# Query projection of a hybrid encoder: feature-major in a 3-pass split instead of token-major in fp32, rotary part through DRAM

## The chip, the cores and the metric

The kernel runs on one core of one Trainium2 chip. The metric is the device time of one execution in microseconds (us). TensorE (PE) multiplies, VectorE (DVE), ScalarE (ACT) and GpSimd (POOL) work element by element, SyncE (SP) issues DMAs; ACT and POOL issue some too. Each engine takes its instructions in the order in which they were written for it, and waits at the first that isn't ready.

## The reference

Two encoder layers for 256 prompt tokens and 8 streams of 16 sample tokens, so 384 token rows. A layer projects its input with `w_in`, feeds three head groups, projects their outputs with `w_out`, and ends in a SwiGLU block. The change touches the queries of group A, latent attention (8 heads, 64 plain and 32 rotary features each):

```python
q = einsum('btr,rf->btf', rmsnorm(cq, mla_q_norm), w_uq).reshape(B, T, 8, 96)
q_nope, q_pe = q[..., :64], rope(q[..., 64:], pos)
# prompt: s = (q_lat . ckv + q_pe . kpe) * 96 ** -0.5, softmax in a block-causal mask
# sample: the same over 256 cached rows and 16 new ones, q_lat = q_nope . w_uk
```

Group B is a gated delta rule (an inverse of small triangular matrices, then a recurrence over four chunks of 64 tokens), group C a convolution of width 31 over 256 channels.

## The kernel before

All activations that are multiplied with big weights stand feature-major, features on partitions and the 384 tokens along the free axis. The big products are made in a split of three passes: `split` writes a high part (fp32r, by ACT) and a low part (the rest, by DVE), and `g3` issues three fp32r matmuls, high x high, low x high and high x low. Small products are plain fp32, which the compiler makes two PE instructions each.

The order of the work is not that of the source. Each section opens with `at('name')`, which adds an offset from the table `PRI` to the priority of what follows, and a scheduler orders each engine's instructions by priority and readiness. `ENG` says which engine makes a copy or issues a DMA. So sections overlap: the convolution's 62 tap instructions a layer (`acc`, section `taps`, one DVE instruction each) are spread over DVE from the moment the convolution input is there until `cpost`.

The names that the prediction uses, in the order of a layer:
- `pt`, `pf`: PE products of `w_in`, token- or feature-major. `cq` is the query input; `ev_cq` takes its mean square (`rcq`, nine small DVE steps for the power of -1/2) and transposes it (`pcq`).
- `Tn`, `pr`: the 15 DVE steps of the triangular inverse; its result goes to DRAM (`scr`, SP) and comes back (`tc`, POOL), then PE products `pL`.
- `py`, `pkS`, `Sn`, `o`, `so`: the chunks of the recurrence; then the sample state's part, `pxs`, `pxt`, `pu`, `po`, `o2s`, `pgo`, `pS`. DVE scales the sample state by one long instruction, `S<-S,gv`.
- `queries(t)`, one for each tile of 128 tokens: six fp32 products `pq` of 384 columns (tokens stationary), a scaling with the norm factor to `qp` (ACT), the rotary part `rp` and `qp` (DVE), eight PE transposes `pqT`, copies to `qT` (ACT). For the sample tile also `qpe` and the products `pqL`.
- `scores` and `values` (`psc`, `mx`, `P`, `pPT`, `ppv`) for the prompt's eight head pairs; `past`, `s_scores` and `s_values` (`ppn`, `pkp`, `pss`, `mxs`, `E`, `Ps`, `pPs`, `poL`) for the eight streams.
- `cy`: the end of the convolution group; then `w_out` (`pw`).

Of the kernel before, what the change touches and what calls it, by code (L numbers as in the profile page):

```python
# [33 lines left out]
def _constants():
# [56 lines left out]
def encoder_step(ctx, tc, I, O):  # L91
# [251 lines left out]
    for L in range(depth):  # L343
# [487 lines left out]
        for t in range(3):  # L831
            pool.memset(kps[t], 0.0)
            if t < 2:
                pool.tensor_copy(kps[t][:, 32 + t:128:64], ctab[:, K_KP:K_KP + 1].to_broadcast([128, 2]))
# [164 lines left out]
        wq = []  # L999
        for k in range(3):  # L1000
            w = stm.tile([128, 1024], F32, name="wq", tag="wlo", bufs=NW)[:, 0:768]
            sp.dma_start(w, I['w_uq'][L][k * 128:k * 128 + 128, :])
            wq.append(w)
        qT = [None] * 3

        def queries(t):
            cT_, r = cqT[t]
            qp = tl(k2p, "qp", 1, 1024, "qp").rearrange("p (a c) -> p a c", a=4)
            e = pool if ENG.get('qpm', 'p') == 'p' else dve
            m = qp[:, :, 96:224].rearrange("p a (b c) -> p a b c", b=2)  # L1010
            e.memset(m[:, :, :, 0:32], 0.0)
            if t < 2:
                e.tensor_copy(m[:, :, :, t], ctab[:, None, K_QP:K_QP + 1].to_broadcast([128, 4, 2]))
            for hf in range(2):
                p = psum("pq", "gg"[hf])
# [337 lines left out]
```

## Time and profile before

| | us |
|---|---|
| median of 3 runs | 1084.95 (1084.43 to 1089.22) |
| the profiled execution, its own time | 1090.11 |
| its span, first to last instruction | 1088.0 |
| PE busy in the span | 1045.5 (96%) |
| DVE, ACT, POOL busy | 633.6 (58%), 470.1 (43%), 75.5 (7%) |
| mean granted TensorE clock | 0.987 of full speed |

The profiled execution took 5.2 us more than the median of the runs, and its span is 2.1 us shorter than its own time. A busy PE counts each matmul from its start to its modelled end, and successive ones overlap. Stages are read below as windows of the span; layer 0's mixing work ends at about 222 us, layer 1's at about 759 us, and the SwiGLU block follows each.

### The profile page before, as it was taken

The page shows a single profiled execution, that of the slowest core. Times are in us where ns is not written, and L with a number is a line of the kernel's source. Part 1 is how long each engine was busy: PE and PEld are TensorE (multiplying, and loading weights), DVE is VectorE, ACT ScalarE, POOL GpSimd, SP SyncE. Part 2 cuts the span into 40 slices and gives each one's busy share as a digit, 9 for nine tenths or more (in the row PEclk, how much of TensorE's full clock was granted, in tenths as well). Part 3 has the DMA queues.
Part 4 walks back from the last instruction along what each step waited for, and adds up shares of the span by engine and source line. Part 5 has one row for each costly group of instructions (what it writes and reads, how often), then busy time and mean ns, then how long its engine had stood idle before and what let it go on. Part 6 is the DMA issues. An engine that isn't in the chain of part 4 may idle for free.

```text
span 1088.0 us, 17535 instructions
## 1 busy us (share of the span) xinstructions
PE 1045.5 (96%) x6620; PEld 918.0 (84%) x6620; DVE 633.6 (58%) x1680; ACT 470.1 (43%) x1116; POOL 75.5 (7%) x152
## 2 busy tenths in 40 slices
PE   7998988999999999999999999999999999999997
PEld 7978656788999999988799786667889999998885
DVE  5577679867444444423666777798655444443336
ACT  5764435544433433323356544455444333433232
POOL 0201310001000000000002012201000000000001
PEclk9999999999999999999999899899999999999999
DMA  8435211342443344443354251124433443334441
GB/s 250 106 94 147 57 29 40 126 149 85 128 143 116 117 119 146 123 135 117 117 167 128 65 154 43 29 48 141 132 116 117 133 138 117 117 123 149 117 140 72
DMA packets 99662, 124.93 MB, mean 115 GB/s; under 512 B 18544, under 2 KB 85782, under 8 KB 99578
## 3 DMA queue, kind: packets, MB, share of 16 engines
q1 hardware_dynamic: 92722, 117.15, 35.7%
q0 software_dynamic: 1792, 5.34, 1.6%
q10 hardware_dynamic: 5064, 1.33, 0.5%
q8 instruction: 52, 0.85, 0.3%
q14 instruction: 32, 0.26, 0.1%
HBM read 117.28 MB, written 6.52 MB: 114 GB/s over the span
## 4 chain that ended last, share of the span: by engine, by line
PE 78%; DVE 9%; DMA 6%; ACT 3%; issue 2%; POOL 1%; POOLq 0%; DVEq 0%; SPq 0%; ACTq 0%
PE pf L182 13%; PE pf L180 13%; PE pf L181 13%; PE pw L182 7%; PE pw L181 7%; PE pw L180 7%; DMA raw<-in_w_in_dram 2%; PE pq L1018 2%; DVE wlo L137 2%; DVE acc L140 1%; PE pxT L194 1%; ACT whi L134 1%; PE poL L1143 1%; PE pss L1119 1%; PE ppv L1088 1%
## 5 line engine op out<-in xcount | busy, mean ns | idle before, releaser
L137 DVE TENSOR_TENSOR wlo<-raw,whi 128x512 fp32r<-128x512 f32 (+3 forms) x364 | 233.6, 662 | 278.3 <-ACT whi L134 277.5
L134 ACT ACTIVATE whi<-raw 128x512 fp32r<-128x512 f32 (+3 forms) x364 | 210.1, 605 | 331.1 <-PE pw L182 96.2
L181 PE MATMUL pf<-x1l,whi 128*128 128x384 f32 (+2 forms) x736 | 245.1, 333 | 0.4 <-DVE x1l L137 0.4
L182 PE MATMUL pf<-x1h,wlo 128*128 128x384 f32 (+2 forms) x736 | 245.0, 333 | 0.0
L180 PE MATMUL pf<-x1h,whi 128*128 128x384 f32 (+2 forms) x736 | 244.8, 333 | 0.0
L181 PEld LDWEIGHTS pf<-x1l,whi 128*128 128x128 f32 x736 | 138.4, 188 | 0.7 <-DVE x1l L137 0.7
L180 PEld LDWEIGHTS pf<-x1h,whi 128*128 128x128 f32 x736 | 138.4, 188 | 0.1
L182 PEld LDWEIGHTS pf<-x1h,wlo 128*128 128x128 f32 x736 | 138.4, 188 | 0.0
L182 PE MATMUL pw<-whi,hl 128*128 128x512 f32 x240 | 94.8, 395 | 0.0
L180 PE MATMUL pw<-whi,hh 128*128 128x512 f32 x240 | 94.8, 395 | 0.0
L181 PE MATMUL pw<-wlo,hh 128*128 128x512 f32 x240 | 94.8, 395 | 0.0
L140 DVE SCALAR_TENSOR_TENSOR acc<-cb,cw,acc 128x384 f32<-128x384 f32 x120 | 70.9, 609 | 0.1
L180 PE MATMUL pf<-xTh,whi 128*128 128x384 f32 (+2 forms) x176 | 57.6, 337 | 1.0 <-ACT whi L134 0.8
L181 PE MATMUL pf<-xTl,whi 128*128 128x384 f32 (+2 forms) x176 | 56.9, 335 | 0.2 <-DVE xTl L137 0.2
L182 PE MATMUL pf<-xTh,wlo 128*128 128x384 f32 (+2 forms) x176 | 56.5, 333 | 0.0
L199 POOL TENSOR_TENSOR lnst<-lnst,ctab 128x1 f32<-128x1 f32 x12 | 11.4, 951 | 642.0 <-DVE lnst L140 642.0
L182 PEld LDWEIGHTS pw<-whi,hl 128*128 128x128 f32 x240 | 45.1, 188 | 10.7
L181 PEld LDWEIGHTS pw<-wlo,hh 128*128 128x128 f32 x240 | 45.1, 188 | 10.7
L180 PEld LDWEIGHTS pw<-whi,hh 128*128 128x128 f32 x240 | 45.1, 188 | 10.4
L137 DVE TENSOR_TENSOR fh<-fs,pf 128x384 f32<-128x384 f32 x44 | 24.4, 554 | 47.2 <-PE pf L182 47.2
L182 PE MATMUL pt<-whi,xTl 128*128 128x264 f32 (+2 forms) x144 | 46.5, 325 | 0.0
L181 PE MATMUL pt<-wlo,xTh 128*128 128x264 f32 (+2 forms) x144 | 46.0, 320 | 0.0
(368 smaller groups left out, 1733.6 us busy)
## 6 DMA issues: line engine op xcount, KB each, us to landing
raw<-in_w_gate_dram SPq DMA_DIRECT2D x44, 512.0 KB, 3.9
raw<-in_w_up_dram SPq DMA_DIRECT2D x44, 512.0 KB, 3.9
raw<-in_w_down_dram SPq DMA_DIRECT2D x44, 512.0 KB, 3.7
raw<-in_w_in_dram SPq DMA_DIRECT2D x20, 512.0 KB, 4.7
raw<-in_w_out_dram SPq DMA_DIRECT2D x16, 512.0 KB, 4.3
pn<-in_cache_mla_ckv_dram SPq DMA_DIRECT2D x16, 256.0 KB, 2.6
raw<-in_w_in_dram SPq DMA_DIRECT2D x8, 384.0 KB, 3.2
wq<-in_w_uq_dram SPq DMA_DIRECT2D x6, 384.0 KB
```

The lines of the kernel that those rows point to most:

```text
L134: act.activation(o, i, AF.Copy)
L137: dve.tensor_tensor(o, a, b, op=op)
L140: dve.scalar_tensor_tensor(o, a, s, b, op0=op0, op1=op1)
L180: mm(out, lh, rh, start=first, stop=False)
L181: mm(out, lh, rl, start=False, stop=False)
L182: mm(out, ll, rh, start=False, stop=last)
L194: nc.tensor.transpose(out, in_, ident[:k, :k])
L199: pool.tensor_tensor(o, i, mhalf.to_broadcast(list(i.shape)), op=OP.pow)
L1018: mm(p[:, 0:384], cT_[:, k * 128:k * 128 + 128], wq[k][:, c], start=k == 0, stop=k == 2)
L1088: mm(po[e * 64:e * 64 + 64, 0:128], V[:, k, vc], PT[:, (e * nt + k) * 128:(e * nt + k) * 128 + 128], start=k == 0, stop=k == nt - 1)
L1119: mm(p[0:64, 0:272], qpe[64:96, b].rearrange("p a t -> p (a t)"), kpp[64:96, :], start=False, stop=True)
L1143: mm(o, pn[:, 0, c], PT[:, 0:128], start=True, stop=False)
```

## The change

The queries are made feature-major, as the big products are. `ev_cq` splits the transposed `cq` into `cqh`, `cql` and `cq2`, without the norm. `q_block` loads a third of `w_uq` (256 columns), scales it with the norm's gain while it is split, and makes two blocks of 128 features over all 384 tokens by `g3`. The first block holds the rotary features of all heads: DVE turns them (`ro`), SP stores both halves to DRAM (`ros`) and loads them back in the layouts that the scores want, four loads into `qx` for the samples and four into `qT` for the prompt. The other two blocks hold the plain features, and ACT copies them to `qs` and `qT`. The norm factor is no longer applied to the queries: it is folded with the scale into the exponential's `scale` (`sr` for the prompt; for the samples `srs`, which POOL brings into its layout by one store and eight loads of single numbers). The eight `pqT` transposes of each tile go. The two `pss` products of 64 outputs each become one of 128. `zz` moves from POOL to DVE, `cy` from DVE to ACT. The table `PRI` is set anew.

```diff
-K_COS, K_SIN, K_KP, K_QP = 1236, 1332, 1428, 1429
-K_N = 1430
+K_COS, K_SIN, K_KP = 1236, 1332, 1428
+K_CF, K_SF = 1429, 1701
+K_N = 1973
...
+    ang = np.arange(272, dtype=np.float32)[None, :] * inv[p % 16][:, None]
+    c[:, K_CF:K_CF + 272], c[:, K_SF:K_SF + 272] = np.cos(ang, dtype=np.float32), np.sin(ang, dtype=np.float32)
...
-    'cv1': 94, 'qkv': -11, 'sat': -1027, 'wout': -2, 'ckv': -82, 'qlat': 26, 'gso': -32, 'pat': 4, 'glu': 15,
+    'cv1': 94, 'sat': -1027, 'wout': -2, 'ckv': -82, 'gso': -32, 'pat': 4, 'glu': -115, 'kvb': 308, 'taps': -7,
...
-    'zz': 'p', 'acc': 'd', 'xld': 'p', 'cqg': 'a', 'ogc': 's', 'scr': 'a', 'okv': 'a', 'gac': 'a', 'kn': 'd',
+    'zz': 'd', 'acc': 'd', 'xld': 'p', 'cqg': 'a', 'ogc': 's', 'scr': 'a', 'okv': 'a', 'gac': 'a', 'kn': 'd',
...
-        cqT = [None] * 3
+        cqb = tl(k1p, "qL", 1, 2048, "cq", F32R)
+        cqh = cqb[:, 0:1152].rearrange("p (k c) -> p k c", k=3)
+        cql = cqb[:, 1152:1920].rearrange("p (k c) -> p k c", k=2)
+        cq2 = tl(k1p, "sp", 4, 384, "cq2", F32R)
+        sr = [None] * 3
+        srs = par.tile([128, 8], F32, name="srs")
+        rsc = drp.tile([128, 1], F32, name="rsc")
+        rosc = [drp.tile([128, 384], F32, name=f"ros{w}") for w in range(2)]
 
         def ev_cq(t, p):
-            cn, cT_ = k15("cqn"), k15("cqT")
+            cn = k15("cqn")
             cp('cqn', cn, p[:, 0:384])
-            r = rms_scale(cn, 384, cT_, "rcq")
+
+            sr[t] = rms_scale(cn, 384 * SCALE ** 2, k15("cqj"), "rcq", 1e-6 / SCALE ** 2)
+            if t == 2:
+                dq('rsd').dma_start(rsc, sr[2])
+                for h in range(8):
+                    dq('rsd').dma_start(srs[16 * h:16 * h + 16], rsc.rearrange("(b t) c -> t (b c)", b=8))
             q = psum("pcq", "K")
             for k in range(3):
                 tr(q[:, k * 128:k * 128 + 128], cn[:, k * 128:k * 128 + 128])
-            for k in range(3):
-                c = slice(k * 128, k * 128 + 128)
-                scl('cqg', cT_[:, c], q[:, c], qg[:, k:k + 1])
-            cqT[t] = (cT_, r)
+            c = slice(t * 128, t * 128 + 128)
+            qv = q[:, 0:384].rearrange("p (k c) -> p k c", k=3)
+            copy(cqh[:, :, c], qv)
+            tt(cql[:, :, c], qv[:, 0:2], cqh[:, 0:2, c].bitcast(F32), OP.subtract)
+            tt(cq2[:, c], qv[:, 2], cqh[:, 2, c].bitcast(F32), OP.subtract)
         tok_major(w_in, C_CQ, 384, xT, ev_cq)
...
+        qT = tl(k2p, "qT", 1, 2048, "qT").rearrange("p (a e c) -> p a e c", a=4, e=2)
+        qs = tl(k2p, "qs", 1, 512, "qs").rearrange("p (a c) -> p a c", a=4)
+        qpe = tl(k1p, "qpe", 1, 512, "qpe").rearrange("p (b e a t) -> p b e a t", b=4, e=2, a=4)
+        for e, r0 in ((0, 96), (1, 32)):
+            pool.memset(qT[r0:r0 + 32, :, e, :], 0.0)
+            pool.memset(qT[r0:r0 + 2, :, e, 0:64], 1.0)
+            pool.memset(qT[r0:r0 + 1, :, e, 128:192], 1.0)
+        wu = I['w_uq'][L].rearrange("(k p) (h c) -> k p h c", p=128, h=8)
...
+        def q_block(h0, nh, c0, n):
+            raw = stm.tile([128, 1024], F32, name="raw", tag="raw", bufs=2)
+            v = raw[:, 0:768].rearrange("p (k h c) -> p k h c", k=3, h=nh)
+            for k in range(3):
+                sp.dma_start(v[:, k], wu[k, :, h0:h0 + nh, c0:c0 + n])
+            h, l = (a[:, 0:768].rearrange("p (k n) -> p k n", k=3) for a in w_slots())
+            for k in range(3):
+                i, oh, ol = v[:, k], h[:, k, :], l[:, k, :]
+                if n == 32:
+                    i = i.rearrange("p h (w c) -> p w h c", w=2)
+                    oh, ol = (o.rearrange("p (w h c) -> p w h c", w=2, h=8) for o in (oh, ol))
+                else:
+                    oh, ol = (o.rearrange("p (h c) -> p h c", h=nh) for o in (oh, ol))
+                act.activation(oh, i, AF.Copy, scale=qg[:, k:k + 1])
+                for w in range(2) if n == 32 else (slice(None),):
+                    stt(ol[:, w], i[:, w], qg[:, k:k + 1], oh[:, w].bitcast(F32), OP.mult, OP.subtract)
+            out = []
+            for m in range(2):
+                p = psum("pq", "g")
+                c = slice(m * 128, m * 128 + 128)
                 for k in range(3):
+                    g3(p[:, 0:384], h[:, k, c], l[:, k, c], cqh[:, k, :], cql[:, k, :] if k < 2 else cq2, k == 0, k == 2)
+                out.append(p[:, 0:384])
+            return out
+        at('q2')
+        p1, p2 = q_block(0, 8, 64, 32)
+        ro = [k15(f"ro{i}") for i in range(4)]
+        for o, i, c in ((ro[0], p1, K_CF), (ro[1], p1, K_SF), (ro[2], p2, K_SF), (ro[3], p2, K_CF)):
+            tt(o[:, 256:384].rearrange("p (b t) -> p b t", b=8), i[:, 256:384].rearrange("p (b t) -> p b t", b=8),
+               ctab[:, None, c + 256:c + 272].to_broadcast([128, 8, 16]), OP.mult)
+            tt(o[:, 0:256], i[:, 0:256], ctab[:, c:c + 256], OP.mult)
+        tt(ro[0], ro[0], ro[2], OP.subtract)
+        tt(ro[1], ro[1], ro[3], OP.add)
+        for w in range(2):
+            dq('qro', 's').dma_start(rosc[w], ro[w])
+        rv = [o.rearrange("(a e i) c -> e i a c", a=4, e=2) for o in rosc]
+        qx = tl(k3p, "k2k", 4, 512, "qx").rearrange("p (h c) -> p h c", h=8)
+        for w in range(2):
+            for g_ in range(2):
+                r0, c0 = 32 * g_ + 16 * w, 256 + 64 * g_
+                dq('qro', 's').dma_start(qx[r0:r0 + 16], rosc[w].rearrange("(h i) c -> i h c", h=8)[:, :, c0:c0 + 64])
+        for i in range(4):
+            cp('qpe', qpe[0:64, i].rearrange("p e a t -> p a e t"),
+               qx[0:64, :, 16 * i:16 * i + 16].rearrange("p (a e) t -> p a e t", a=4), 'p')
+        for e in range(2):
+            for w in range(2):
+                r0 = 64 * (1 - e) + 16 * w
+                dq('qro', 's').dma_start(qT[r0:r0 + 16, :, e, :], rv[w][e][:, :, 0:256])
+        for u in range(2):
+            for m, p in enumerate(q_block(4 * u, 4, 0, 64)):
+                cp('qsn', qs[:, 2 * u + m, :], p[:, 256:384])
                 for e in range(2):
+                    cp('qpn', qT[e * 64:e * 64 + 64, 2 * u + m, e, :], p[e * 64:e * 64 + 64, 0:256])
...
-                mm(pv[:, e, :], qT[t][:, a, e, :], Kb[:, a, e, 0:n])
+                mm(pv[:, e, :], qT[:, a, e, t * 128:t * 128 + 128], Kb[:, a, e, 0:n])
-            ts(mx[:, 1, :], mx[:, 0, :], -SCALE, None, OP.mult)
+            ts(mx[:, 1, :], mx[:, 0, :], sr[t], -1.0, OP.mult, OP.mult)
...
+                act.activation(P_[:, e, :], pv[:, e, :], AF.Exp, bias=mx[:, 1, e:e + 1], scale=sr[t],
...
-            mm(p[0:64, 0:272], qpe[64:96, b].rearrange("p a t -> p (a t)"), kpp[64:96, :], start=False, stop=True)
-            mm(p[64:128, 0:272], qpe[0:32, b].rearrange("p a t -> p (a t)"), kpp[0:32, :], start=False, stop=True)
+            rb = slice(32 * (b // 4), 32 * (b // 4) + 32)
+            mm(p[:, 0:272], qpe[rb, b % 4].rearrange("p e a t -> p (e a t)"), kpp[rb, :], start=False, stop=True)
...
+            act.activation(E[:, 0:272], p[:, 0:272], AF.Exp, bias=mx[:, 1:2], scale=srs[:, b:b + 1], accum_out=mx[:, 2:3])
```

Where the table and the new code put things, at three places of layer 0.

PE, from the sample state's products to the first score product; before, as the compiled program lists them (line, operation, output and inputs, shape, repeats):

```order
L769 MATMUL pxs<-QK_142,S_1142 64x32 x16
L194 MATMUL pgo<-ctab,o_1055 128x128
L1018 MATMUL pq<-wq,cqT 128x384
L194 MATMUL pxt<-ctab,xs 128x128 x4
L1018 MATMUL pq<-wq,cqT 128x384 x2
L788 MATMUL pu_1192<-R_1188,T_968 64x64 x8
L1018 MATMUL pq<-wq,cqT 128x384
L795 MATMUL po_1203<-U_1201,aa 64x64 x8
L1048 MATMUL pqL<-qT,ukT 128x128 x3
```

And the same place now:

```order
L773 MATMUL pxs<-QK_142,S_1142 64x32 x16
L198 MATMUL pgo<-ctab,o_1055 128x128
L198 MATMUL pxt<-ctab,xs 128x128 x4
L792 MATMUL pu_1192<-R_1188,T_968 64x64 x8
L799 MATMUL po_1203<-U_1201,aa 64x64 x8
L1106 MATMUL psc<-Kb,qT 128x128 x4
L198 MATMUL pgo<-ctab,o2s 128x128
L818 MATMUL pS_1236<-U_1201,Kp 64x64
```

All query products now stand ahead of `pxs`, among the chunks of the recurrence; nothing is left between `pxs`, `pxt`, `pu` and `po`, and the first scores follow `po` at once.

SP, from the stores of the turned features to the last of their loads, now (before, this queue held only `pk`, `pn` and `out_gdn` here):

```order
L1064 DMA ros_1310<-ro_1978 128x384
L1071 DMA qx<-ros_1309 16x8x64
L1138 DMA pk<-in_cache_mla_kpe_dram 128x2x32 x3
L1071 DMA qx<-ros_1309 16x8x64
L1140 DMA pn<-in_cache_mla_ckv_dram 128x2x256
L759 DMA out_gdn_prompt_dram<-Sn 64x2x64 x2
L1071 DMA qx<-ros_1310 16x8x64 x2
L1078 DMA qT<-ros_1309 16x4x256
L1078 DMA qT<-ros_1310 16x4x256
L1138 DMA pk<-in_cache_mla_kpe_dram 128x2x32
L1078 DMA qT<-ros_1309 16x4x256
L1140 DMA pn<-in_cache_mla_ckv_dram 128x2x256
```

The loads stand among `pk` and `pn`, whose buffers come free as the recurrence goes on; the fourth `qT` load stands behind the last `pn` shown, which waits for `po`.

POOL, around the inverse, now (before, `kp` and `tc` followed `Tn` directly):

```order
L604 DMA ad<-scr 96x256
L607 MEMSET Tn 96x256
L608 MEMSET Tn 96x16
L890 DMA rsc<-rcq 128x1
L892 DMA srs<-rsc 16x8x1 x8
L836 MEMSET kp_6641 128x128
L838 COPY kp_6641<-ctab 128x2
L625 DMA tc<-scr_639 128x4x32
```

Nine DMAs were put between the inverse's start and the load of its result.

## Rows read from the trace of the kernel before

**Rows 1.** Page, part 1: busy us, share of the span, instructions.

```profile
PE 1045.5 (96%) x6620; PEld 918.0 (84%) x6620; DVE 633.6 (58%) x1680; ACT 470.1 (43%) x1116; POOL 75.5 (7%) x152
```

**Rows 2.** Windows (start:end, length, busy us of each engine, clock, DMA), both layers.

```profile
115.00:152.50 37.50, 34.43 (x320) 23.15 (x316) 28.79 (x84) 14.70 (x41) 9.72 (x18) 1.00 0.16 40
...
657.00:694.60 37.60, 35.34 (x297) 24.14 (x298) 27.49 (x83) 14.42 (x39) 8.72 (x17) 0.91 0.16 41
```

**Rows 3.** Windows from the sample state's scaling to cy, both layers.

```profile
152.50:222.00 69.50, 64.70 (x482) 45.98 (x482) 58.44 (x184) 36.18 (x120) 8.55 (x24) 0.98 0.25 72
694.60:758.90 64.30, 61.84 (x485) 44.62 (x486) 58.10 (x183) 35.57 (x118) 8.74 (x24) 1.00 0.26 75
```

**Rows 4.** Timeline of PE, layer 0: start us, us, what, count.

```profile
162.97 0.63 PE L194 MATMUL pqT<-ctab,qp 128*128 128x128 f32 x4 [0.52 <-DVE qp L137]
163.44 0.81 PE L1018 MATMUL pq<-wq,cqT 128*128 128x384 f32 x2
164.09 0.38 PE L1063 MATMUL psc<-Kb,qT 128*128 128x128 f32 x2
```

**Rows 5.** Timeline of PE, fp32r matmuls of 384 columns in a dense stretch.

```profile
299.82 0.34 PE L180 MATMUL pf<-x1h,whi 128*128 128x384 f32 x1
300.00 0.34 PE L181 MATMUL pf<-x1l,whi 128*128 128x384 f32 x1
```

**Rows 6.** Groups by line and shape, PE: count, busy us, mean ns.

```profile
L1018 PE MATMUL pq<-wq,cqT 128*128 128x384 f32 x72 | 31.0, 549 | 0.1
...
L194 PE MATMUL pqT<-ctab,qp 128*128 128x128 f32 x48 | 8.8, 295 | 0.7 <-DVE qp L137 0.5 <-DVE r L140 0.2
```

**Rows 7.** Timeline of PE, one stream's score products.

```profile
178.43 0.62 PE L1118 MATMUL pss<-kk,qL 128*128 128x272 f32 x2
178.98 0.44 PE L1119 MATMUL pss<-kk,qpe 32*64 32x272 f32 x1
...
179.59 0.33 PE L194 MATMUL pqT<-ctab,qp 128*128 128x128 f32 x1
```

**Rows 8.** Groups by line and shape, DVE.

```profile
L140 DVE SCALAR_TENSOR_TENSOR rp<-pq,rcq,ctab 128x64 f32<-128x64 f32 x24 | 5.9, 275 | 0.0
L137 DVE TENSOR_TENSOR aa<-pAA,Dm 128x256 f32<-128x256 f32 x12 | 4.9, 422 | 2.6 <-PE pAA L570 2.4
L140 DVE SCALAR_TENSOR_TENSOR rp<-pq,rcq,ctab 128x128 f32<-128x128 f32 x12 | 4.1, 344 | 1.6 <-ACT qp L157 1.6
```

**Rows 9.** Chain that ended last, layer 0: start us, us, what.

```profile
158.12 0.64 PE po L795 x16
...
161.12 1.31 POOL so L199
```

**Rows 10.** DMA issues: KB each, us to landing.

```profile
pk<-in_cache_mla_kpe_dram SPq DMA_DIRECT2D x16, 32.0 KB, 1.9
```

**Rows 11.** Timelines: last rcq step and first tc load, both layers.

```profile
83.26 0.15 DVE L140 SCALAR_TENSOR_TENSOR rcq<-rcq 128x1 f32<-128x1 f32 x1
94.96 0.79 POOL L621 DMA_DIRECT2D tc<-scr  x1
...
627.29 0.15 DVE L140 SCALAR_TENSOR_TENSOR rcq<-rcq 128x1 f32<-128x1 f32 x1
636.30 0.79 POOL L621 DMA_DIRECT2D tc<-scr  x1 [16.46 <-DVE rp L140]
```

**Rows 12.** Windows: DMA at the start; PE at a low clock.

```profile
10.00:20.00 10.00, 9.15 (x53) 8.56 (x53) 7.12 (x17) 5.64 (x12) 0.87 (x2) 1.00 0.86 254
...
590.00:600.00 10.00, 7.85 (x49) 7.21 (x48) 6.67 (x24) 6.50 (x17) 1.25 (x2) 0.99 0.62 156
600.00:610.00 10.00, 10.00 (x58) 7.96 (x60) 3.67 (x10) 5.99 (x25) 0.00 (x0) 0.67 0.26 74
```

**Rows 13.** Timeline of PE, in the last of these windows.

```profile
601.01 0.52 PE L180 MATMUL pt<-whi,xTh 128*128 128x384 f32 x1
601.33 0.52 PE L181 MATMUL pt<-wlo,xTh 128*128 128x384 f32 x1
```

More of the change, by code (lines that the diff above doesn't have):

```diff
@@ L106, in encoder_step @@
     BANKS = {"g": 3, "G": 3, "K": 2}
-    SMALL = {"Gs": 22, "Ks": 12, "Ms": 4, "Ls": 6}
+    SMALL = {"Gs": 21, "Ks": 14, "Ms": 4, "Ls": 6}
     turn = [0, 0]
@@ L833, in encoder_step @@
             if t < 2:
[L834 removed]
+                pool.tensor_copy(kps[t][:, 33 - t:128:64], ctab[:, K_KP:K_KP + 1].to_broadcast([128, 2]))
         def rope(o, i, t, n, r=1.0):
@@ L998, in encoder_step @@
         at('uq')
[L999 to L1015, printed above, removed]
-                for k in range(3):
-                    c = slice(hf * 384, hf * 384 + 384)
-                    mm(p[:, 0:384], cT_[:, k * 128:k * 128 + 128], wq[k][:, c], start=k == 0, stop=k == 2)
-                pv = p[:, 0:384].rearrange("p (h c) -> p h c", h=4)
-                for e in range(2):
-                    scl('qpn', qp[:, 2 * hf:2 * hf + 2, e * 192:e * 192 + 64], pv[:, e:4:2, 0:64], r)
-                rope(qp[:, 2 * hf:2 * hf + 2, 64:192].rearrange("p a (e c) -> p a e c", e=2)[:, :, :, 0:32],
-                     pv[:, :, 64:96], t, 4, r)
-            qT[t] = tl(k2p, "qT", 2, 1024, "qT").rearrange("p (a e c) -> p a e c", a=4, e=2)
-            for j in range(2):
-                p = psum("pqT", "K")
-                for a in range(2):
-                    for e in range(2):
-                        tr(p[:, (a * 2 + e) * 128:(a * 2 + e) * 128 + 128], qp[:, 2 * j + a, e * 128:e * 128 + 128])
-                cp('qT', qT[t][:, 2 * j:2 * j + 2], p.rearrange("p (a e c) -> p a e c", a=2, e=2))
@@ L1035, in encoder_step @@
         at('qlat')
         qL = tl(k1p, "qL", 1, 2048, "qL").rearrange("p (k b c) -> p k b c", k=2, b=8)
-        qpe = tl(k1p, "qpe", 1, 512, "qpe").rearrange("p (b a t) -> p b a t", b=8, a=4)
-        for e, rows in ((0, slice(64, 96)), (1, slice(0, 32))):
-            cp('qpe', qpe[rows].rearrange("p b a t -> p a b t"),
-                             qT[2][rows, :, e, :].rearrange("p a (b t) -> p a b t", b=8), 'p')
         for j in range(2):
@@ L1108, in past @@
             for k in range(2):
-                tr(p[0:96, k * 128:k * 128 + 128], pk[:, k, :])
-            cp('kpp', kpp[0:96, 0:256], p[0:96, 0:256])
-            cp('kpp2', kpp[0:96, 256:272], kpT[0:96, 256 + 16 * b:272 + 16 * b], 'p')
+                tr(p[0:32, k * 128:k * 128 + 128], pk[:, k, :])
+            rb = slice(32 * (b // 4), 32 * (b // 4) + 32)
+            cp('kpp', kpp[rb, 0:256], p[0:32, 0:256])
+            cp('kpp2', kpp[rb, 256:272], kpT[0:32, 256 + 16 * b:272 + 16 * b], 'p')
             cp('kt2', kt[:, :, 256:272], cTs[:, :, 16 * b:16 * b + 16], 'p')
@@ L1118, in s_scores @@
             mm(p[:, 0:272], qL[:, 1, b, :], kt[:, 1, :], start=False, stop=False)
-            mm(p[0:64, 0:272], qpe[64:96, b].rearrange("p a t -> p (a t)"), kpp[64:96, :], start=False, stop=True)
-            mm(p[64:128, 0:272], qpe[0:32, b].rearrange("p a t -> p (a t)"), kpp[0:32, :], start=False, stop=True)
+            rb = slice(32 * (b // 4), 32 * (b // 4) + 32)
+            mm(p[:, 0:272], qpe[rb, b % 4].rearrange("p e a t -> p (e a t)"), kpp[rb, :], start=False, stop=True)
             mx = small(4, "Ms", "mxs")
             dve.tensor_reduce(mx[:, 0:1], p[:, 0:272], axis=AX.X, op=OP.max)
-            ts(mx[:, 1:2], mx[:, 0:1], -SCALE, None, OP.mult)
+            ts(mx[:, 1:2], mx[:, 0:1], srs[:, b:b + 1], -1.0, OP.mult, OP.mult)
             E = tl(glp, "gx", 1, 512, "E")
-            act.activation(E[:, 0:272], p[:, 0:272], AF.Exp, bias=mx[:, 1:2], scale=SCALE, accum_out=mx[:, 2:3])
+            act.activation(E[:, 0:272], p[:, 0:272], AF.Exp, bias=mx[:, 1:2], scale=srs[:, b:b + 1], accum_out=mx[:, 2:3])
             dve.reciprocal(mx[:, 3:4], mx[:, 2:3])
```

23 lines of the change are left out of this document (6 added, 17 removed), and 14 rows, old and new, of tables (ENG, PRI).

## The prediction

> **What bounds the kernel now.** I read the page first. PE is busy 96% of the span, DVE 58% [rows 1], so the kernel looks PE-bound, and most of it is: the SwiGLU block runs fp32r matmuls back to back, a 384-column one every 0.18 us [rows 5]. The change touches only the mixing part of each layer, so I cut that into two stages by windows. Stage A, the recurrence, runs from the scaling of `zz` to the instruction `S<-S,gv`: 37.5 us in layer 0 with PE busy 34.4 and DVE 28.8, 37.6 us in layer 1 with 35.3 and 27.5 [rows 2]. Stage B runs from there to `cy`: 69.5 and 64.3 us, PE busy 64.7 and 61.8, DVE 58.4 and 58.1 [rows 3]. The reader is to see that in stage B two engines are close to full. DVE does nearly the same 58 us in both layers, and has only 11.1 us (layer 0) and 6.2 us (layer 1) of idle time left; whatever PE gives up there, the stage cannot get shorter than DVE's work.
>
> **PE, per layer.** Removed: 18 fp32 products of 384 columns, two instructions each. Two instructions take 0.65 us from start to the next start (163.44 to 164.09), so 18 x 0.65 = 11.7. And 24 transposes `pqT`, four in 0.47 us (162.97 to 163.44): 2.8 [rows 4]. Added: 3 blocks x 2 halves x 3 k x 3 passes = 54 fp32r matmuls at 0.18 = 9.7 [rows 5]. The rotary `pss` products: four instructions in 0.61 us (178.98 to 179.59) become two of the size of the `pss` just before them, 0.55 for two (178.43 to 178.98) [rows 7]: 8 x 0.06 = 0.5 less. Net 11.7 + 2.8 + 0.5 - 9.7 = 5.3 us of PE a layer, 11 in all. From the other side: the groups' busy time, which counts the waits for weights and the low-clock stretches too, is 31.0 + 8.8 = 39.8 for both layers [rows 6]; less 19.4, and with the 1.0, that is 21.4. So PE's own relief is 11 to 21 us.
>
> **DVE, per layer.** Removed: `rp`, 6 x 0.344 + 12 x 0.275 = 5.4, and 6 sums to `qp`, 128 wide like the wider `rp`, at most 6 x 0.344 = 2.1 [rows 8]. Added: 13 instructions of 128 columns (low parts of the rotary block and of `cq2`, four `ro`) at 0.344 = 4.5; 16 of 256 columns (low parts, four `ro`, three `cql`, three `zz`) at 0.422 = 6.8; two sums of 384, at an estimated 0.5 from these two rows, 1.0. Net 12.3 - 7.5 = 4.8 us more DVE a layer. Where it lies decides: all the new work stands in stage A or before it, two thirds of the removed work (tiles 0 and 1, 5.0 us) stood in stage B. The order puts some taps and weight splits behind `S<-S,gv` in its place, so stage B's DVE work falls by 0 to 5; I take 2.
>
> **Stage A.** PE gets all 54 products (9.7) in place of the eight products and eight transposes (0.65 x 8 + 0.9 = 6.1) that the order of before had there: +3.6 on 34.4 of 37.5. DVE goes from 28.8 to at most 28.8 + 12.3 - 2.5 = 38.6, less the taps that wait. The recurrence is a chain across engines and the new products fill its gaps. Between nothing and the whole +3.6, I take +1 a layer.
>
> **Stage B.** Layer 0: DVE 58.4 - 2 = 56.4. PE gets lighter, so I let its idle time fall from 11.1 to layer 1's 6.2: 62.6, a gain of 6.9. Layer 1: 56.1 + 5.5 = 61.6, a gain of 2.7, as its idle time has little left to give.
>
> **What is put on the queues.** The constants grow by 543 columns of 128 x 4 bytes, 278 KB, into a stretch where the DMA engines are 86% busy at 254 GB/s [rows 12]: +1.1 us, once. The round trip of the turned features: SP waits for the store to land before it issues the first load; a small DMA lands in 1.9 us [rows 10], so store and load cost about 4 us, plus SP's waits. In layer 0 the fourth `qT` load stands behind a `pn` that waits for `po`. `po` takes from 158.12 to 158.76 [rows 9], so with two issues ahead of it and 1.9 to land this load is there at about 161 to 162, and the scores behind `po`, with `pgo` and `pS` queued behind them on PE, wait for it. But `pgo` needs the power on POOL, which starts only at 161.12 and takes 1.31 [rows 9]: PE would wait there anyway. I cost it at nothing; if that cover were gone it would be 3 us, once. ACT loses about as much copying as it gains and is busy about half of stage B [rows 3]: nothing. The nine DMAs on POOL, see the third rival: nothing, at most 9.5 a layer.
>
> **Sum.** +1 +1 - 6.9 - 2.7 + 1.1 = -6.5, rounded to -7. That is made against the profiled execution, 1090.11 with 2.1 of it outside the span; its stages, not what lies around them, change, so the same 7 us come off the median: 1084.95 - 7 = **1078**. This case runs from -3 to -12.
>
> **Rivals.**
>
> *PE is the bound everywhere, and the whole relief is gained*: -11 to -21, so 1064 to 1074. For it speaks the 96% [rows 1]; against it DVE's 58 us in stage B, which would have to run with almost no idle time: 11.1 + 6.2 + 4 = 21 is the most that both layers' idle time and a lighter DVE could give.
>
> *DVE and the chain hide it*: no change, 1082 to 1087. DVE has 4.8 us a layer more, and stage A would have to take it. The 64.3 us of layer 1 stand on 58.1 of DVE [rows 3]; if no idle time goes, only the 2 us of moved work are left, and stage A gives them back. The Trainium skill (Perfetto Trace Analysis, section Identifying the Most-Contended Engine) says that a matmul's busy share tells little of how far TensorE is from its limit, and has one read the share of its weight loads beside the other engines' occupancy. By that rule PE's 46.0 of 69.5 stands below DVE's 58.4, DVE would be the bound of stage B, and the time would come out at this rival's; the trace agrees in that order of the two, but PE's own waits there are not visible in either number.
>
> *The inverse comes late, and the kernel is slower*: POOL's nine DMAs stand ahead of `tc`. `rsc` waits for the last `rcq` step, `srs` for `rsc` to land; behind them wait `kp` and `tc`, and behind `tc` the products `pL` and the whole recurrence. Price: nine issues at 0.79 plus a landing of 1.9 = 9.0, some 9.5 with waits. From the last `rcq` to the first `tc` there are now 11.5 us in layer 0 and 8.9 in layer 1 [rows 10, 11]. So it is free if `rcq` ends as early as now, and decides when `rcq` slips by over 2 us in layer 0, or at all in layer 1. In the new order `rcq` ends by the third or fourth of the 15 `Tn` steps, earlier against `Tn` than before, which speaks against it. Lost in full in both layers: -7 + 19 = 1097; in part, 1090 to 1097.
>
> *PE's clock falls where the fillers went*: between `pxs` and `pgo` PE now waits. PE was busy 7.85 us of 590 to 600, and in 600 to 610 the granted clock is 0.67 [rows 12]; there a 384-column fp32r matmul starts every 0.32 us, not 0.18, which is the level of 1.2 GHz [rows 5, 13]. If the first 5 us of stage B's scores ran at that level in both layers, it would cost about 2.5 each; if the 54 products did, 54 x 0.14 = 7.6 a layer. Time: 1083 to 1093. The Trainium skill (TensorE: Matmul & The Clock Gate, Part 1) has the idle state at half the clock, released by activity; the trace's two levels agree.
>
> **Chances.** My case 0.50, the whole PE relief 0.12, no change 0.18, the late inverse 0.10, the clock 0.10. Faster by over 0.5% (5.4 us, about what a measurement of this kernel tells from no change) takes four fifths of my case and all of the second, and a little more from single stages: 0.55. Slower: the late inverse and half of the clock case, 0.16. The rest, 0.29. The range must leave out no more than two in ten: it takes in the second case, my own and no change, and the clock case in part, 1064 to 1088, and leaves out the late inverse and the rest of the clock case. My case's own range is 1073 to 1082.
>
> **What would show each step.** 54 `pq` matmuls a layer spaced 0.18 us and no `pqT`: PE. A stage B of 62 to 63 us in both layers with DVE's busy time 55 to 58: the main step; a stage B that falls to 55 with DVE full would show the second case. Stage A one us longer: the fill. The first `tc` load more than 10 us behind the last `rcq` step, with `pL` waiting: the third rival. A wait of PE for `qT` behind `po` of more than 3 us: the cover I assumed is wrong. Wrong altogether would be a change outside these stages, in the SwiGLU block or in the products of `w_in`, which the new table also moves and which I costed at nothing.

## The result, and the profile after

The changed kernel takes 1098.19 us (median; 1091.71 to 1103.99), the kernel before 1084.69 in the same session: a ratio of 1.0118, 95% interval 1.0080 to 1.0156. So it is 8.7 to 16.9 us slower, where 7 us less was forecast. The profiled execution took 1097.87 us, span 1096.1. In what follows a ratio leaves out any execution that took over 1.5% more than the fastest of its kernel (one each in x1, x10 and x11); the medians hold them.

The first rows are the two stages of the prediction in the kernel after, by windows with the columns of [rows 2, 3]: stage A of both layers, then stage B.

```profile
120.60:158.70 38.10, 36.51 (x350) 27.79 (x350) 28.89 (x85) 20.10 (x56) 6.48 (x11) 0.97 0.22 60
665.10:702.10 37.00, 33.40 (x328) 25.57 (x328) 28.16 (x84) 19.08 (x53) 5.46 (x9) 0.96 0.24 66
...
158.70:232.30 73.60, 64.37 (x447) 47.33 (x449) 59.03 (x173) 33.36 (x104) 6.94 (x20) 0.85 0.29 89
702.10:771.20 69.10, 62.59 (x435) 45.88 (x436) 57.28 (x171) 33.70 (x104) 7.80 (x20) 0.85 0.26 78
```

Stage A is as long as it was (+0.6 and -0.6 us). Stage B is 4.1 and 4.8 us longer than in [rows 3], where -6.9 and -2.7 were forecast: with 35 and 50 PE instructions fewer, a DVE as busy as before, and a mean granted clock of 0.85, not 0.98 and 1.00. And stage A begins late: at 120.6 instead of 115.0 in layer 0, at 665.1 instead of 657.0 in layer 1. The stretches behind `cy` give some back (232.3 to 665.1 is 432.8 us, before 435.0; behind 771.2 it is 324.9, before 329.1); the rows don't show by what. In all +8.1 us of span.

**The late start.** POOL's timeline of both layers, from the store of the norm factors to the first load of the inverse (start, length, engine, line, operation, idle time before and what ended it):

```profile
84.38 0.58 POOL L890 DMA_DIRECT2D rsc<-rcq  x1 [4.95 <-DVE pr L141]
93.64 4.32 POOL L892 DMA_DIRECT2D srs<-rsc  x8 [8.68 <-DMA rsc<-rcq]
...
98.85 0.78 POOL L625 DMA_DIRECT2D tc<-scr  x1 [0.43 <-issue]
...
626.96 0.57 POOL L890 DMA_DIRECT2D rsc<-rcq  x1 [4.79 <-DVE Tn L615]
635.52 4.22 POOL L892 DMA_DIRECT2D srs<-rsc  x8 [7.98 <-DMA rsc<-rcq]
642.41 0.78 POOL L625 DMA_DIRECT2D tc<-scr  x1 [2.67 <-DMA scr<-T]
```

`rcq` is done about as early as before, but POOL waits 8.7 and 8.0 us for a store of 512 bytes, and `tc` is issued at 98.85 and 642.41 instead of 94.96 and 636.30 [rows 11]. In layer 1 what `tc` waits for last is not POOL's queue but the inverse's result: `scr`, issued at 636.49, had still to land; the median landing of that store is 5.4 us here, and 2.1 in x1 below, which keeps the order. POOL is not the only engine that waits. These are ACT's and then PE's timeline of layer 0, behind the same store; the 512 KB of `w_in` for that `whi` were issued at 86.94:

```profile
97.56 0.63 ACT L138 ACTIVATE whi<-raw 128x512 fp32r<-128x512 f32 x1 [7.77 <-DMA raw<-in_w_in_dram]
```

```profile
99.79 0.45 PE L198 MATMUL pck<-ctab,kp 128*128 128x128 f32 x1 [3.09 <-ACT kp L138]
99.89 0.67 PE L185 MATMUL pf<-xTl,whi 128*128 128x384 f32 x1
100.35 0.52 PE L186 MATMUL pf<-xTh,wlo 128*128 128x384 f32 x1
100.67 0.52 PE L184 MATMUL pf<-xTh,whi 128*128 128x384 f32 x1
```

The load needed 10.6 us, its median over the program is 4.1. Everything queued on ACT behind the waiting `whi`, `kp` among it, came late; PE stood still for 3.1 us, and the `pf` behind that start every 0.32 us, the spacing of the lower clock [rows 13]. In layer 1 ACT waits 8.06 us there, PE 3.63.

**The bare chain.** This is PE's timeline in stage B of layer 1, then the same place in the kernel before:

```profile
705.97 1.12 PE L799 MATMUL po<-U,aa 64*64 64x64 f32 x16
707.02 1.22 PE L1106 MATMUL psc<-Kb,qT 128*128 128x128 f32 x4
713.97 0.47 PE L198 MATMUL pgo<-ctab,o2s 128*128 128x128 f32 x1 [5.73 <-DVE o2s L141]
714.38 1.13 PE L818 MATMUL pS<-U,Kp 32*64 32x64 f32 x32
...
721.55 1.11 PE L1159 MATMUL pss<-kk,qL 128*128 128x272 f32 x2
```

```profile
698.35 0.68 PE L795 MATMUL po<-U,aa 64*64 64x64 f32 x16
...
700.46 1.46 PE L1018 MATMUL pq<-wq,cqT 128*128 128x384 f32 x4
701.75 0.60 PE L194 MATMUL pqT<-ctab,qp 128*128 128x128 f32 x4
702.18 2.75 PE L1018 MATMUL pq<-wq,cqT 128*128 128x384 f32 x8
705.23 0.44 PE L194 MATMUL pgo<-ctab,o2s 128*128 128x128 f32 x2 [0.30 <-DVE o2s L137]
```

From `po` to `pgo` it is a chain over DVE, ACT and POOL, 6.9 us before and 8.0 now. Before, query products ran in it, and PE waited 0.3 us behind them. They are gone, the chain is not: PE waits 5.7 us with nothing to do. What the trace grants PE around it, by windows of 2 us, three in each layer, with the columns of [rows 2] (PE's busy time comes second, the clock is the third number from the end):

```profile
154.00:156.00 2.00, 0.80 (x12) 0.49 (x11) 2.00 (x6) 1.40 (x5) 0.75 (x2) 1.00 0.00 0
158.00:160.00 2.00, 1.93 (x19) 1.40 (x15) 1.22 (x1) 0.94 (x3) 0.00 (x0) 0.50 0.00 0
178.00:180.00 2.00, 2.00 (x9) 1.60 (x9) 1.48 (x3) 0.23 (x1) 0.00 (x0) 0.50 0.85 145
...
696.00:698.00 2.00, 0.32 (x6) 0.13 (x4) 1.61 (x4) 1.77 (x7) 1.82 (x5) 1.00 0.09 29
700.00:702.00 2.00, 2.00 (x39) 1.94 (x37) 0.68 (x2) 0.00 (x0) 0.00 (x0) 0.50 0.00 0
720.00:722.00 2.00, 2.00 (x16) 1.31 (x12) 1.48 (x4) 1.35 (x6) 0.00 (x0) 0.50 0.00 0
```

From 156.8 to 180.7 and from 699.5 to 723.4 the clock is 0.50, the lower of its two levels: 23.9 us in each layer. In the kernel before, the low stretches near that place were 3.4 and 6.8 us long. The wait for `o2s` can't have started it: in layer 1 that wait begins at 708.2, and the clock had fallen at 699.5. What stands ahead of the fall is a PE short of work just before `pxs`, busy 0.80 and 0.32 of the 2 us shown, as no query product was left to fill its wait for `o`. Low from there on, it held through the chain.

Who waits for that PE is seen on DVE. These are DVE's waits in stage B, layer 0 and layer 1, and then layer 1 in the kernel before (us in all, times, longest):

```profile
DVE mxs L1164 <- PE pss L1162: 2.6, 2, 2.2
DVE mx L1108 <- PE psc L1106: 2.3, 3, 1.6
...
DVE mxs L1164 <- PE pss L1162: 3.8, 4, 1.6
DVE S L141 <- PE pS L818: 1.3, 1, 1.3
```

```profile
DVE mxs L1122 <- PE pss L1120: 1.0, 4, 0.4
```

DVE's idle time in stage B is 14.6 and 11.8 us, before 11.1 and 6.2. Its waits for `pss`, `psc` and `pS` alone are 4.1 us longer in layer 0 (6.0, before 1.9) and 3.6 in layer 1 (5.1, before 1.5). Not all of that lies at the low clock: the longest single waits for `pss`, 2.2 us at 226 and 1.6 at 767, stand at the end of the streams, at 1.00.

### The profile page after: what moved, and what is told of

Same layout as the page of the kernel before. It is cut to its first block, busy times and chain, and to the rows that moved or that the text cites. A ratio compares the mean times of both kernels' runs of the same rounds, so it can differ in the third digit from the quotient of the medians.

```text
span 1096.1 us, 17477 instructions
## 1 busy us (share of the span) xinstructions
PE 1041.3 (95%) x6576; PEld 921.8 (84%) x6576; DVE 639.5 (58%) x1686; ACT 475.6 (43%) x1114; POOL 81.5 (7%) x158
## 4 chain that ended last, share of the span: by engine, by line
PE 77%; DVE 8%; DMA 7%; ACT 4%; issue 2%; POOL 1%; SPq 0%; ACTq 0%; POOLq 0%; DVEq 0%
PE pf L185 13%; PE pf L184 12%; PE pf L186 12%; PE pw L186 7%; PE pw L184 7%; PE pw L185 7%; DMA raw<-in_w_in_dram 3%; DVE acc L144 2%; DVE wlo L141 1%; PE pxT L198 1%; ACT whi L138 1%; PE pss L1162 1%; PE ppn L198 1%; PE ppv L1131 1%; PE psc L1106 1%
## 5 line engine op out<-in xcount | busy, mean ns | idle before, releaser
L184 PE MATMUL pf<-xTh,whi 128*128 128x384 f32 (+2 forms) x176 | 60.3, 344 | 1.2 <-ACT whi L138 1.2
L185 PE MATMUL pf<-xTl,whi 128*128 128x384 f32 (+2 forms) x176 | 60.6, 345 | 0.2 <-DVE xTl L141 0.2
L186 PE MATMUL pf<-xTh,wlo 128*128 128x384 f32 (+2 forms) x176 | 60.4, 345 | 0.0
L184 PE MATMUL pt<-whi,xTh 128*128 128x264 f32 (+2 forms) x144 | 45.8, 318 | 0.0
```

The lines of the kernel that those rows point to most:

```text
L184: mm(out, lh, rh, start=first, stop=False)
L185: mm(out, lh, rl, start=False, stop=False)
L186: mm(out, ll, rh, start=False, stop=last)
```

## The experiments

Each is compared with the kernel before on its own chip. The scheduler decides the order, so most edits move other instructions too; where every engine's order was kept, the text says so.

**x1_spread.** The same order as the change.

```diff
-        rsc = drp.tile([128, 1], F32, name="rsc")
+        rsc = drp.tile([128, 128], F32, name="rsc")
...
-                dq('rsd').dma_start(rsc, sr[2])
+                dq('rsd').dma_start(rsc[:, 0:1], sr[2])
```

> The change with one edit: the 128 norm factors that are stored to DRAM, 4 bytes from each partition, land 512 bytes apart instead of side by side in one 512-byte line; every engine's order stays what it was. Theory A (the store itself is slow, because 128 pieces of 4 bytes go into the same few DRAM lines, and it holds up the load of w_in behind it): the landing of rsc falls from 9.0 and 8.3 us to about 2, the load of w_in issued 2.6 us after it lands in 4 to 5 instead of 10.6 us, ACT's wait of 7.8 us goes, and the time falls by 10 to 14 us to 1084 to 1088. Theory B (4-byte pieces are slow wherever they go): landing still 8 to 9 us, 1096 to 1100. Theory C (the store is not the cause, the half clock behind the recurrence is): time within 3 us of the change, whatever the landing does.

Measured 1091.41 us, ratio 1.0080 (1.0041 to 1.0118). POOL's timeline, layer 0:

```profile
84.83 0.58 POOL L890 DMA_DIRECT2D rsc<-rcq  x1 [4.24 <-DVE pr L141]
86.87 4.20 POOL L892 DMA_DIRECT2D srs<-rsc  x8 [1.46 <-DMA rsc<-rcq]
```

The store lands within 2.0 us, ACT's wait for `w_in` is gone in layer 0 and 2.1 us at most in layer 1, and the first `pL` follows the last `rcq` after 17.8 and 16.6 us, not 22.4 and 22.8 (before: 16.8 and 14.0). So theory A's mechanism is right, but the time falls by half of what it asked, to above its range. The 1.0 and 2.6 us up to `pL` that are left against the kernel before are not the store's landing. The bare chain stands unchanged: `pgo` still waits 8.1 us for `o2s`, and the clock is low for 20.5 us in each layer.

**x2_row** and **x3_sel**: the store in pieces of 512 bytes, and no DMAs at all but a matmul with a 0/1 matrix.

```diff
...
+                ts(cj[:, 0:128], ctab[:, K_ONE:K_ONE + 128], sr[2], None, OP.mult)
-                dq('rsd').dma_start(rsc, sr[2])
+                dq('rsd').dma_start(rsc, cj[:, 0:128])
```

```diff
...
+        ts(sl[:, 144:152], ctab[:, K_IND + 2:K_IND + 10], sr[2], None, OP.mult)
+        mm(p[:, 0:8], sl[:, 0:128], sl[:, 144:152])
+        copy(srs, p[:, 0:8])
```

> The change with the norm factor copied along 128 columns first, so that each partition stores 512 bytes in one piece rather than 4; the scheduler orders the rest a little differently. Theories A and B alike: rsc lands in about 2 us, the load of w_in behind it is not held up, the first pL of layer 0 comes at 99 to 101 us instead of 106.5, and the time falls by 10 to 14 us. Theory C: the time stays at 1095 to 1100 because the store cost nothing.

> The change without the nine DMAs on POOL: the factors are spread over the partitions by one fp32 matmul with a 0/1 matrix, just ahead of the latent queries, and three small DVE instructions for it. Theories A and B: no ACT wait over 4 us for w_in, pL of layer 0 at 99 to 101 us and of layer 1 at 641 to 643 us, time 1084 to 1088, and the half clock behind the recurrence stays. Theory C: 1095 to 1100. If the time falls below 1080, the half clock also hung on the nine DMAs.

1096.37 us (1.0106; 1.0052 to 1.0160) and 1099.75 (1.0141; 1.0097 to 1.0185). In x2 the store lands in 2 us as well, in x3 there is none, `pL` comes at 104.6 and 102.2, later than expected, and yet earlier than the change's 106.5; and nothing is gained. In x3 the new order takes it: PE waits 13.5 us for `o2s` and 9.5 for `o` (the change: 8.1 and 4.2). In x2 these two waits are as in the change, and what took it there is open; the median clock of its executions is 0.966, where that of x1 is 0.972. By their time alone these two would have spoken for theory C; they show that an edit that lets the scheduler choose anew can't price a part of some 6 us.

**x4_before_dmas** and **x9_before_dmas_spread**: the kernel before with the nine DMAs, side by side and 512 bytes apart. The two have the same order.

```diff
+        srs = par.tile([128, 8], F32, name="srs")
+        rsc = drp.tile([128, 1], F32, name="rsc")
...
             r = rms_scale(cn, 384, cT_, "rcq")
+            if t == 2:
+                dq('rsd').dma_start(rsc, r)
+                for h in range(8):
+                    dq('rsd').dma_start(srs[16 * h:16 * h + 16], rsc.rearrange("(b t) c -> t (b c)", b=8))
```

> The kernel before with nothing but the nine DMAs added (the store of the last rcq, and the eight loads, which nothing reads), at the place where the change has them. Theories A and B: rsc lands in 8 to 9 us here too, a load of w_in that is issued behind it is held up, and the time rises by 8 to 14 us to 1093 to 1099. Theory C: within 3 us of the kernel before, 1083 to 1088.

> The kernel before with the nine DMAs of x4_before_dmas (1099.05 us), and the 128 stored numbers 512 bytes apart instead of side by side; every engine's order is that of x4_before_dmas, which is not quite that of the kernel before. Theory A (128 pieces of 4 bytes into one 512-byte line are slow and hold up the loads behind them): rsc lands in under 5 us and the time falls by 6 to 14 us to 1085 to 1093. Theory O (the DMAs cost nothing themselves; what costs is the order that the scheduler makes of a program that has them): 1096 to 1102.

1099.05 us (1.0133; 1.0083 to 1.0182) and 1081.95 (0.9992; 0.9960 to 1.0024). POOL's timeline in layer 1, of x4 and of x9:

```profile
632.46 0.57 POOL L880 DMA_DIRECT2D rsc<-rcq  x1 [7.88 <-DVE Tn L611]
641.19 4.21 POOL L882 DMA_DIRECT2D srs<-rsc  x8 [8.16 <-DMA rsc<-rcq]
```

```profile
617.59 0.57 POOL L880 DMA_DIRECT2D rsc<-rcq  x1 [7.88 <-DVE Tn L611]
619.60 4.26 POOL L882 DMA_DIRECT2D srs<-rsc  x8 [1.44 <-DMA rsc<-rcq]
```

x9 came out below theory A's range. The nine DMAs as such cost nothing that shows (0.9992, give or take 3.5 us, in an order that is not quite that of the kernel before); where the 128 numbers land makes the whole difference, 15 us here (1.0133 less 0.9992, of 1084.7; give or take 6). Theory O falls.

**x5_fill6** and **x6_fill_early**: idle matmuls behind `po`, six, or four in `pgo`'s tile and twelve.

```diff
+        for _ in range(6):
+            mm(p[:, 256:512], ident, ctab[:, K_ONE:K_ONE + 256])
         tt(o2, o2, p[:, 0:256].rearrange("p (h d) -> p h d", h=4), OP.add)
```

> The change with six idle fp32 matmuls (identity by ones, 256 columns, into columns of po's PSUM tile that nobody reads) put right behind po in each layer, where PE waits 2.3 and 5.7 us for o2s; 12 in all. Theory K (the gap that the moved pq products left behind lets PE's clock fall to half for 23.9 us in each layer, and the work behind it is slow by that): the half-clock stretch behind pxs shortens to under 14 us in each layer, PE's wait for o2s is filled rather than lengthened, and the time falls by 4 to 10 us to 1088 to 1094. Theory L (the chain on DVE, ACT and POOL sets the length there, PE's clock does not matter): the stretch may shorten, but the time stays at 1095 to 1101.

> The change with four such matmuls in the PSUM tile of the last prompt pgo and twelve behind po in each layer. This makes the scheduler take pxs early, and leave 10 to 12 pq products, pV, pK and the latent queries pqL for the stretch between pxs and the last pgo, as the kernel before had them. Theory K: the half-clock stretch of 23.9 us shrinks to under 8 us, PE waits under 1 us for o2s, and the time falls by 8 to 14 us to 1084 to 1090. Theory L: 1095 to 1101. If the twelve idle matmuls lie on the path themselves, 12 x 0.45 = 5 us a layer are lost again and the time is 1090 to 1098.

1103.79 us (1.0170; 1.0121 to 1.0219) and 1095.22 (1.0100; 1.0066 to 1.0134). I had placed them ahead of the sum that reads `po`, in the same tile, and the sum waited for them: in x5 PE waits 12.7 us for `o2s`, not 8.1. They lay on the path themselves, so neither run says anything on the clock: x5 came out above both theories' ranges, and x6 is in theory L's and in that for matmuls on the path. x6 was worth it for its order, which x11 takes up.

**x7_old_table** and **x8_before_new_table**: only the table `PRI` exchanged.

> The change with the table of priorities of the kernel before (names that it lacks count 0). It still has all pq products ahead of pxs and nothing but some pqL between pxs and po, so that PE has as little to do behind po. Theory T (the new table is the cause): 1078 to 1085. Theory K with the store's theory A (the nine DMAs and the empty gap are the cause, both are still here): 1092 to 1102, rsc lands in over 8 us, and a half-clock stretch of over 15 us stands behind pxs.

> The kernel before with the new table of priorities. It keeps its fp32 query products and their transposes, and has no rsc store. It still has pq and pqT behind po. Theory T: 1092 to 1100. Theories A and K: within 5 us of the kernel before, 1080 to 1089, with no half-clock stretch over 10 us behind pxs.

1120.14 us (1.0336; 1.0276 to 1.0396) and 1103.00 (1.0159; 1.0091 to 1.0228). Theory T falls on x7: without its table the change is 24 us slower still. But both came out above every range that I gave them: the new table is bad for the old code (from the first `pL` to the first `py`, 21.8 us in layer 1 instead of 14.2). A table belongs to its code, and neither run prices one part of it.

**x10_spread_fill_behind**: x1 with the six idle matmuls of x5, behind the sum that reads `po`.

> x1_spread (1091.4 us) with six idle fp32 matmuls behind po in each layer, placed behind the sum that reads po, so that the chain through o2s need not wait for them, as it did in x5_fill6. Theory K (the half clock in the gap costs): the half-clock stretches behind pxs, 20.5 us in each layer of x1_spread, fall to under 12, and the time falls by 3 to 8 us to 1083 to 1088. Theory L (the chain sets the length, the clock does not matter): 1089 to 1096.

1091.28 us (1.0054; 1.0025 to 1.0082). Of PE's waits in x1, then in x10 (in all, times, longest):

```profile
PE pgo L198 <- DVE o2s L141: 8.1, 2, 5.7
```

```profile
PE pgo L198 <- DVE o2s L141: 2.6, 2, 1.6
```

PE's wait is filled, and nothing is gained against 1091.41, as theory L had it. That doesn't show that the wait was no loss: the six matmuls can delay what stands behind them. On the clock the run says less than it was to: the low stretch went from 20.5 us to 13.7 and 6.8 in layer 0, and to 10.2 and 3.4 in layer 1, so it did not shorten in the one and by a third in the other.

**x11_spread_early_pxs**: x1 with one idle matmul in the tile of the last prompt `pgo`. The scheduler then takes that PSUM bank, and with it `pxs`, early.

```diff
             p = psum("pgo", "G")
+            if t == 1:
+                mm(p[:, 256:512], ident, ctab[:, K_ONE:K_ONE + 256])
```

> x1_spread (1091.4 us) with a single idle matmul in the PSUM tile of the last prompt pgo, in each layer. It makes the scheduler take that bank, and so pxs, some 8 us earlier, and leaves real products (pq, pV, pK, puk, pqL) between pxs and the last pgo. Theory K: no half-clock stretch over 7 us behind pxs, a wait of PE for o2s under 2 us, and 1080 to 1086. Theory L: the gap behind po is filled but nothing is gained, as the chain on DVE is as long as before: 1088 to 1095.

1080.75 us (0.9968; 0.9934 to 1.0003). From the scaling of `zz` to the first `pss`, and from there to `cy`, by windows of the change and of x11, layer 0:

```profile
120.60:176.70 56.10, 47.55 (x465) 35.74 (x465) 43.39 (x126) 24.70 (x72) 7.93 (x13) 0.82 0.19 50
176.70:232.30 55.60, 53.34 (x332) 39.38 (x333) 44.53 (x133) 28.76 (x88) 5.49 (x18) 0.96 0.35 109
```

```profile
117.80:168.80 51.00, 44.66 (x468) 34.14 (x469) 39.52 (x115) 23.15 (x64) 8.74 (x13) 0.90 0.22 56
168.80:223.80 55.00, 52.73 (x357) 38.61 (x355) 48.32 (x148) 32.35 (x99) 6.47 (x18) 1.00 0.26 76
```

`pxs` starts at 143.2, not 155.8, while the last chunk and the query products still run. The chain behind it is as long as ever (PE waits 8.7 us for `o2s`), but begins earlier, and the streams with it. The two theories divide the marks: the time lies in theory K's range and 7 us below theory L's, but K's wait, under 2 us, was missed, and the low stretch is 10.2 us in layer 0 and still 20.5 in layer 1. Clock and place move together here: up to the first `pss` the clock is low for 10.1 and 9.1 us in x11, and for 19.9 and 22.0 in the change. In layer 1 that part falls by 8.2 us (56.4 to 48.2), and 7.9 are given back in the streams (49.7 to 57.6), where the low clock now reaches 11.4 us into them, not 1.9. So bringing `pxs` ahead is what gained; whether by the place of the chain or by the clock, this run doesn't tell.

**x12_sel_early_pxs**: x3 with the same matmul.

> x3_sel (no rsc and srs DMAs, 1099.75 us, half clock for 34 and 24 us behind pxs) with the same single idle matmul, which again brings pxs ahead and leaves real products behind it. Theory K: the half-clock stretches fall under 8 us and the time falls by 12 to 20 us to 1080 to 1088. Theory L: 1094 to 1100.

1089.63 us (1.0044; 1.0010 to 1.0077), 10 us less than x3: the same gain on another base, between the two theories' ranges. The low stretches fell from 34.1 and 23.9 us to 17.1 and 13.7, so again both moved.

**x13_early_pxs_side_by_side**: x11 with the store of the change; the same order as x11.

> x11_spread_early_pxs (1080.75 us) with the 128 stored numbers side by side again, as the change has them; every engine's order is that of x11. Theory A at the size of the pair x4 and x9 (17 us): 1095 to 1100. Theory A at the size of the pair of the change and x1_spread (7 us): 1086 to 1090. If the store's price were only the order of the other runs: 1079 to 1083. With x11, x1 and the change it also says what bringing pxs ahead is worth with the store as it was: 10 us, if the two causes are independent.

1090.22 us (1.0042; 1.0006 to 1.0077). POOL's timeline, layer 1:

```profile
631.61 0.57 POOL L893 DMA_DIRECT2D rsc<-rcq  x1 [5.78 <-DVE Tn L615]
639.19 4.59 POOL L895 DMA_DIRECT2D srs<-rsc  x8 [7.02 <-DMA rsc<-rcq]
```

1090.22 us is at the edge of the range for theory A's smaller size. The store costs 0.74% here (1.0042 less 0.9968), 8.0 us, 4.1 in the order of the change (1.0118 less 1.0080), each give or take 6. Bringing `pxs` ahead gains 12.1 us with the spread store (1.0080 less 0.9968), 8.2 with the other. Over both pairs: the store 6 us, the chain 10, each give or take 4; together they take the change from 1.0118 to 0.9968.

This pair also prices the clock once. In x13 the clock was low from 271.8 to 282.0, in the SwiGLU block, and in x11 not. The same 41 matmuls there (the windows count three that reach in as well), x13, then x11:

```profile
271.74:282.15 10.41, 10.41 (x44) 10.41 (x43) 2.77 (x4) 4.56 (x7) 0.00 (x0) 0.51 0.34 102
```

```profile
268.37:273.99 5.62, 5.62 (x44) 5.62 (x43) 1.38 (x2) 3.21 (x5) 0.00 (x0) 1.00 0.39 112
```

4.8 us are lost in 10.2 at the lower clock. What brought the clock down there is not shown, so part of what parts these two traces need not be the store's.

**x14_spread_early_pxs_go2**: x11 with `'go2': -987`, as before.

> x11_spread_early_pxs (1080.75 us) with one number of the table put back to that of the kernel before, the one of the last norm and gate of the recurrence (go2, from -19 to -987), so that both last pgo come together, ahead of pS. If the exposed chain behind the recurrence is what is left to lose, as theory L has it: PE's wait for o2s falls from 8.7 to under 6 us and the time to 1074 to 1079, which is below both kernels. If not: 1079 to 1084.

1083.46 us (0.9998; 0.9968 to 1.0029): not better than x11, though PE's wait for `o2s` fell from 8.7 us to 1.0. So that wait is not what is left to lose, and theory L's test fails. The first `pss` comes 2.3 and 2.1 us earlier against `zz`, and in layer 0 the streams take 64.8 us up to `cy` instead of 55.0.

## Why the prediction was wrong, step by step

**PE's own account was right, its effect wrong.** 54 `pq` a layer, spaced 0.17 to 0.18 us, no `pqT`; PE's busy time falls by 4.2 us over the whole kernel although it ran longer at the lower clock. But the step "PE gets lighter, so I let its idle time fall from 11.1 to layer 1's 6.2" failed: DVE's idle time in stage B rose to 14.6 and 11.8 us. The products that went had been PE's filling ahead of `pxs` and in the chain through `po`, `o2s` and `pgo`. Without them PE ran short of work there, its clock was 0.50 for 23.9 us a layer, and DVE waited longer for what PE makes, in part at that level. I read the idle time off the stage as a whole, and not off the place at which the products stood: there PE's wait for `o2s` was 0.3 us because they were in it. That moving them is the cause is shown by x11, x12 and x13, which leave products behind `pxs` again and gain 12, 10 and 8 us on three bases, in orders that differ in other places too. How much of it is the chain and how much the clock is not separated by any run.

**DVE.** Forecast 4.8 us a layer more, measured 3.0 (633.6 to 639.5 for both). The added instructions took 12.2 (forecast 12.3), the removed ones 7.1 (7.5); two removals were not counted, the first step of `cy`, now on ACT, 1.3 a layer, and the copies to `qpe`, now on POOL, 0.8. In stage B DVE was busy 59.0 and 57.3 us: the fall by 2 that I took did not come.

**Stage A.** Forecast +1 each, measured +0.6 and -0.6. Right: the recurrence took in 54 products.

**The nine DMAs.** Costed at nothing, "so it is free if `rcq` ends as early as now". `rcq` did end about as early, and it was not free. The wrong term is the landing: I took 1.9 us for `rsc`, from a small load [rows 10], and it took 9.0 and 8.3. The third rival named the wait and the bound of 1097, with a chance of 0.10; it did not see that the load of `w_in` and, in layer 1, the store of `scr` behind it are held up too, the first with ACT and PE behind it. x4 and x9 settle the cause: 128 stores of 4 bytes side by side, not their number or POOL's queue. The Trainium skill (DMA: Bandwidth & Descriptors, section Why small descriptors are slow) puts the price of small pieces down to a fixed overhead for each packet and the metadata of each descriptor. Both layouts have 128 pieces of 4 bytes, so by that alone they would land alike, and the measurement, 8.7 us against 2.0 from the store's issue to the first load's in layer 1 of x4 and x9 (8.5 against 3.2 in layer 0), says otherwise.

**The round trip of the turned features.** In layer 0 PE waited 2.4 us for the fourth `qT` load and, behind it, 2.3 more for `o2s`. So the cover held: by these rows, without the first wait the second would have been the longer one. The constants, 1.1 us in the forecast: the first `pssq` of layer 0 comes 0.8 us later (38.1 to 38.9).

**The clock.** The sum had it at nothing. The fourth rival had it fall at this place, for 5 us at 2.5 a layer, with a chance of 0.10; the low stretch was 23.9 us, and the price of 2.5 in 5 is what x13 and x11 show in a dense stretch, 4.8 in 10.2. What it cost in stage B can't be had from one trace, as PE is idle in part of it. But each execution's mean granted clock was recorded. The change's four are, in us and clock, 1091.71 at 0.978, 1097.87 and 1098.51 at 0.970, 1103.99 at 0.964. Within one and the same kernel, over 168 executions of the kernels above, 0.01 of clock goes with 9 us (8 to 13 in each of the kernels with nine or more executions). The medians are 0.970 for the change and 0.992 for the kernel before. By this estimate the lower clock goes with some 20 us, more than the whole loss of 13.5, and at an equal clock the change would lead by some 7. It is a correlation and no experiment: what delays an execution can also lower its clock, and the figure goes beyond the clocks that either kernel showed.

The estimate takes in a part of the store's price too: x4's median clock is 0.981 where x9's is 0.990. But it speaks against leaving the clock out of the account of x11 (0.979, where x1 has 0.972).

**What is left.** With both causes taken out, x11 stands 3.5 us below the kernel before (7.2 below to 0.3 above), half of the forecast 7 and not safely faster, so the sizes of the forecast's gains are not confirmed. Why no more comes of a PE that has 5 us a layer less to do: x11's clock is still 0.979, not 0.992, and in x11 and x14 what is gained ahead of the first `pss` is partly lost in the streams up to `cy`. What sets the end of that stretch was not tried. Nor does any run price the new table apart from its code.

## What to carry to other kernels

Before counting a removed instruction as time, look at what stands around it on its engine: where work fills a wait for other engines, taking it out leaves the wait, and can, as here, leave TensorE so short of work that it goes on at half its clock. Compare the mean clock of two kernels, and of the executions of each, before explaining their difference by waits alone. Don't price a DMA by another of like size: look how its pieces lie in DRAM, and which loads are queued behind it. And where a scheduler reorders the whole kernel at each edit, compare pairs that keep the order, since a new order alone cost or gained more here than the part in question.
